# First norm's sums by token on ScalarE, rotary tables by token at the head: one change to a two-layer decoder trunk

## The chip, the cores and the metric

The kernel runs on one core of one Trainium2 chip. The metric is device time in microseconds of one execution of the whole program; a median over runs is given where there are several. Engines are named as in the profile: PE is TensorE, DVE is VectorE, ACT is ScalarE, POOL is GpSimd, SP is SyncE, which here only issues DMAs.

## What is computed

A decoder trunk of two layers over 512 tokens of width 1024, all positions at once, in fp32:

```
for i in range(2):
    h = rms_norm(x, norm_mix[i])
    proj = h @ w_in[i]            # split into parts A, B, C
    y_a = gated_delta_net(...)    # 4 heads of 64, causal conv of width 4
    y_b = mlstm(...)              # 4 heads of 64
    y_c = sliding_window_attention(..., cos, sin)   # 8 q heads, 2 kv heads
    x = x + concat(y_a, y_b, y_c) @ w_out[i]
    x = x + relu(rms_norm(x, norm_mlp[i]) @ w_up[i])**2 @ w_down[i]
    x = x + sigmoid(rms_norm(x, norm_ple[i]) @ w_ple_gate[i]) * (p[i] @ w_ple_proj[i])
return rms_norm(x, norm_final)
```

Two pieces matter here. `rms_norm` needs, for every token, the sum of the squares of its 1024 features. The rotary tables are cos and sin of position times frequency, with 8 frequencies; they turn the first 16 of the 64 features of each q and k head, and are the same in both layers.

## The kernel before

The residual is kept by feature: `X` is eight tiles of 128 features x 512 tokens, loaded from `xT` (L317, 256 KB each). Every fp32 product runs as three matmuls of high and low halves (`mm3`, L161): weights come from `wfm` in chunks of 256 KB (`w_load_`, L135) into the two buffers of `raw`, ACT rounds the high half (L141), POOL or DVE takes the difference (L143). A layer runs as follows.

- **Token-major projections** (tile `tok`, L313 to L319, `tok_mm`): for each of eight feature tiles, X is split into `xsh` (ACT, L190) and `xsl` (DVE, L191), a weight tile of 200 KB is loaded from `wtm` into the same two `raw` buffers (L260) and split into `whi` (ACT, L262) and `wlo` (DVE, L264), and PE issues 12 matmuls of 128x400.
- **First norm** (`Norm`, L194 to L226): `add` squares each X tile on ACT (L201, L204) and sums the squares over the eight tiles into `acc`, the first five sums on POOL and the last two on DVE (L205). `finish` sums over the 128 partitions by matmuls with a column of ones (tile `ss`, L212), works out rT = 1/sqrt(mean) with some ten tiny DVE operations of 128x4, and broadcasts it to all partitions as `R` (L220, L223). In layer 0 `add` is called in L321; later norms add while their X tiles are produced.
- **Gates, rows, conv** (L343 to L455): small DVE chains on the gate columns, then six projections for part A, each followed by a conv on DVE (tiles `craw`, `cc`).
- **Part A**: norms of k (tiles `psst`, `ssq`, `rk`, `cA`), decays, triangular systems (`At`), 16x16 inverses as a serial chain on DVE (`px`), doubling by small matmuls (the first is `t1p`, L564), scan over four blocks.
- **Part B** (`mql`, `mkS`, `me`, `pnm`), then **the rotary tables**, in layer 0 only (`rope_tables`, L231, called in L765): the positions are broadcast to 128 partitions x 512 tokens, and DVE works out the angle and its reduction for sin and cos on full 128x512 tiles (18 DVE operations); ACT's Sin follows (L248), and the tables go to DRAM (`rope_d`, L251). Both layers load them (L767, L770), multiply by R on POOL, and use them in `rope` (L775): shuffle and product on DVE, product and sum on POOL.
- **Part C**, output gates, output projection, then MLP and per-layer embedding, which are long runs of matmuls.

The order on each engine is not written by hand. A planner takes all instructions, ranks them by their place in the program, moved by offsets (`hp_` lifts by 200 places, `PRI` moves whole sections), and lays out a fixed order for each engine from durations of its own. On the chip each engine then runs its list in that order. All loads that this change touches go through SP's one queue.

Of the kernel before, what the change touches and what calls it, by code (L numbers as in the profile page):

```python
# [18 lines left out]
T = 512  # L19
D = 1024  # L20
# [6 lines left out]
# scheduling priority of (section, layer)  # L27
# [12 lines left out]
# columns of the packed constants  # L40
# [6 lines left out]
C_N = 552  # L47
# columns of the packed small weights of a layer
# [13 lines left out]
def trunk(ctx, tc, xT, pT, pos, wfm, wtm, consts, negi, smalls, gfin, out, dbg=None, depth=L):  # L62
# [41 lines left out]
    sc = cst[:, C_SC:C_SC + 8]  # L104
    for l in range(1, depth):
        nc.sync.dma_start(out=sm[l], in_=smalls[l])
# [63 lines left out]
    def rsqrt(y, x, shape, pool, tag):  # L170
        t = pool.tile(shape, F32, tag=tag + "w", name=tag + "w", bufs=2)
        V.tensor_scalar(t.bitcast(I32), x.bitcast(I32), 1, None, ALU.logical_shift_right)
        V.tensor_scalar(y.bitcast(I32), t.bitcast(I32), -1.0, MAGIC, ALU.mult, ALU.add)
        # one step of third order (8/3 too large), then one of Newton's that takes the factor back
        V.tensor_tensor(t, y, y, ALU.mult)
        V.tensor_tensor(t, t, x, ALU.mult)
        V.scalar_tensor_tensor(t, t, -10.0 / 3.0, t, ALU.add, ALU.mult)
        V.scalar_tensor_tensor(y, t, 5.0, y, ALU.add, ALU.mult)
        V.tensor_tensor(t, y, y, ALU.mult)
        V.scalar_tensor_tensor(t, t, -27.0 / 1024.0, x, ALU.mult, ALU.mult)  # L180
        V.scalar_tensor_tensor(y, t, 9.0 / 16.0, y, ALU.add, ALU.mult)
# [11 lines left out]

    class Norm:  # L194
        def __init__(self):
            self.acc = tp.tile([128, T], F32, tag="acc", name="acc", bufs=1)
            self.n = 0
# [10 lines left out]
        def finish(self, pt_=None):  # L208
            pt_ = pt_ or ps_tile
            ps = pt_([128, NB], "ss")  # L210
            for b in range(NB):
                PE.matmul(out=ps[:, b:b + 1], lhsT=self.acc[:, b * 128:(b + 1) * 128], rhs=ones[:, 0:1],  # L212
                          start=True, stop=True)
            ms = tp.tile([128, NB], F32, tag="ms", name="ms", bufs=2)
            V.tensor_scalar(ms, ps, 1.0 / D, EPS, ALU.mult, ALU.add)
            rT = tp.tile([128, NB], F32, tag="rT", name="rT", bufs=2)
            rsqrt(rT, ms, [128, NB], tp, "rn")
            pr = pt_([128, T], "rb")
            for b in range(NB):
                PE.matmul(out=pr[:, b * 128:(b + 1) * 128], lhsT=rT[:, b:b + 1].broadcast_to([128, 128]), rhs=ident,  # L220
                          start=True, stop=True)
            R = tp.tile([128, T], F32, tag="R", name="R", bufs=1)
            A.activation(out=R, in_=pr, func=ACTF.Copy)  # L223
            ri = tp.tile([128, NB], F32, tag="ri", name="ri", bufs=2)
            V.tensor_tensor(ri, ms, rT, ALU.mult)
            return rT, ri, R  # L226

# [1 line left out]
    rope_d = dp.tile([2, 128, T], F32, name="rope_d", bufs=1)  # L229

    def rope_tables(us):  # L231
        pi = us([128, T], "pi").bitcast(I32)
        nc.sync.dma_start(out=pi, in_=pos.broadcast_to([128, T]))
        ang = us([128, T], "ang")
        V.tensor_copy(ang, pi)
        V.tensor_scalar(ang, ang, sc[:, 0:1], None, ALU.mult)
        for dst, off in ((1, 0.0), (0, 0.25)):
            k = us([128, T], "k")
            V.tensor_scalar(k, ang, float(np.float32(1.0 / (2 * np.pi))), off, ALU.mult, ALU.add)
            V.tensor_scalar(k, k, ROUND, ROUND, ALU.add, ALU.subtract)  # L240
            r = us([128, T], "r")
            V.scalar_tensor_tensor(r, k, -PI2[0], ang, ALU.mult, ALU.add)
            for c in PI2[1:]:
                V.scalar_tensor_tensor(r, k, -c, r, ALU.mult, ALU.add)
            if off:
                V.tensor_scalar(r, r, float(np.float32(np.pi / 2)), None, ALU.add)
            V.tensor_scalar(r, r, PI_LO, -PI_LO, ALU.min, ALU.max)
            A.activation(out=k, in_=r, func=ACTF.Sin)  # L248
            if dst:
                V.tensor_scalar(k, k, sc[:, 1:2], None, ALU.mult)  # L250
            nc.sync.dma_start(out=rope_d[dst], in_=k)  # L251
            dump(("rope_c", "rope_s")[dst], k)
# [23 lines left out]
    nrm = Norm()  # L276

    for l in range(depth):
# [33 lines left out]
        # token-major projections: mv, sv, gates  # L312
        pst = [(ps_tile if b < 2 else pa_tile)([128, 400], "tok") for b in range(NB)]  # L313
        for k in range(8):
            if l == 0:
                with hp_():
                    nc.sync.dma_start(out=X[k], in_=xT[k])  # L317
                    XS[k] = split(X[k], xs, "xs", 18, s_l[:, S_GMIX + k:S_GMIX + k + 1])
            tok_mm(pst, k, *tok_weights(l, k))  # L319
        if l == 0:  # L320
            for m in range(8):  # L321
                nrm.add(m)
        with hp_():
            rT, rI, R = nrm.finish(pa_tile)
        dump(f"R{l}", R)
# [52 lines left out]
        # rows  # L378
# [45 lines left out]
        # GDN q, k, v: conv, silu  # L424
# [55 lines left out]
        # k, v token-major  # L480
# [13 lines left out]
        # decays and the lower-triangular systems  # L494
# [41 lines left out]
        # base inverses of 16 x 16, then 32 x 32  # L536
# [78 lines left out]
        # scan over blocks  # L615
# [83 lines left out]
        # c'_{J,I}: ig - bl + totals of blocks J..I-1  # L699
# [64 lines left out]
        if l == 0:  # L764
            rope_tables(us)  # L765
# [231 lines left out]
        if final:  # L997
            # the last row tiles by halves of the tokens, so that the first half's norm hides
# [66 lines left out]
def const_arrays():  # L1065
# [9 lines left out]
    d = i % 64  # L1075
    inv = np.float32(500000.0) ** (-np.arange(0, 16, 2, dtype=np.float32) / np.float32(16))
    cst[:, C_SC] = np.where(d < 16, inv.astype(np.float32)[d % 8], 0.0)
    cst[:, C_SC + 1] = np.where(d < 8, -1.0, np.where(d < 16, 1.0, 0.0))
# [9 lines left out]
def stationary(w, ks, ms):  # L1088
    # [K, M] -> tiles [128 (k), 128 (m)] in the order of use
# [7 lines left out]
def pack(x, p, positions, w_in, conv_w, gdn_a_log, gdn_dt_bias, gdn_norm, mlstm_i_bias, mlstm_f_bias, mlstm_norm,  # L1097
         attn_sinks, w_out, norm_mix, norm_mlp, w_up, w_down, norm_ple, w_ple_gate, w_ple_proj, norm_final):
    def a(v):
        return np.asarray(v)  # L1100

    xT = np.ascontiguousarray(a(x)[0].T.reshape(8, 128, T))
    pT = np.ascontiguousarray(a(p)[:, 0].transpose(0, 2, 1).reshape(L, 2, 128, T))
    pos = np.ascontiguousarray(a(positions).reshape(1, T))
# [42 lines left out]
    return dict(xT=xT, pT=pT, pos=pos, wfm=np.stack(fms), wtm=np.ascontiguousarray(np.stack(tms)), consts=cst, negi=neg,  # L1147
# [3 lines left out]
NAMES = ["xT", "pT", "pos", "wfm", "wtm", "consts", "negi", "smalls", "gfin"]  # L1151
# [17 lines left out]
```

## Time and profile before

| what | value |
|---|---|
| median of 3 runs | 1396.97 us (1394.41 to 1399.37) |
| profiled execution, first to last instruction | 1397.6 us |
| PE busy | 1352.9 us of it |
| DVE, ACT, POOL busy | 839.1, 599.4, 325.1 us |
| moved by DMA | 130.04 MB |

The profiled execution's own time is its span; nothing around it is recorded. A row of the timeline holds the start and the duration in us, engine, line, operation, tile written <- tiles read, and the engine's idle time before it with what ended it. In a row of groups, the numbers behind the bar are busy time in us and mean ns of one. A busy PE is not PE at its peak: the rows also show the TensorE clock that was granted.

### The profile page before, as it was taken

To read this page: it belongs to the slowest core of one execution; us is meant where nothing else is said; L and a number is where in the kernel's file an instruction comes from. 1 tells how busy PE (TensorE), PEld (TensorE's weight loads), DVE (VectorE), ACT (ScalarE), POOL (GpSimd) and SP (SyncE) were. 2 spreads that over 40 slices of the span, in tenths; PEclk is the share of its full clock that TensorE was granted. 3 is DMA by queue.
4 is the path that set the end of the run, shared out by engine and by line. 5 is a ranking of instruction groups with operands and counts; after the bars stand their busy time and mean duration, and the time that the engine had idled before them with its cause. 6 is when DMAs were issued, how large, how long until landed. Compare 5 with 4: busy or idle time off the path is not lost.

```text
span 1397.6 us, 20344 instructions
## 1 busy us (share of the span) xinstructions
PE 1352.9 (97%) x7334; PEld 1113.3 (80%) x7334; DVE 839.1 (60%) x1749; ACT 599.4 (43%) x1236; POOL 325.1 (23%) x302
## 2 busy tenths in 40 slices
PE   7999899999999999999999899999999999999996
PEld 7667788778888888888896678887888888888886
DVE  6877978674344444454758688886544434444555
ACT  5374354254243242443535545634433324234443
POOL 4443632362000000010235455326400000000112
PEclk9999989999999999999999999999999999999998
DMA  4333222233333333332433322212333333233332
GB/s 152 99 99 89 55 57 77 69 98 98 98 99 95 95 97 98 99 98 91 142 106 99 108 69 63 78 54 91 99 98 98 97 99 95 95 98 98 98 98 76
DMA packets 88596, 130.04 MB, mean 93 GB/s; under 512 B 21408, under 2 KB 30112, under 8 KB 88496
## 3 DMA queue, kind: packets, MB, share of 16 engines
q1 hardware_dynamic: 87408, 127.71, 30.0%
q8 instruction: 57, 0.93, 0.3%
q10 hardware_dynamic: 1088, 1.05, 0.2%
q14 instruction: 43, 0.35, 0.1%
HBM read 123.18 MB, written 5.54 MB: 92 GB/s over the span
## 4 chain that ended last, share of the span: by engine, by line
PE 80%; DVE 9%; ACT 3%; issue 3%; POOL 2%; DMA 1%; SPq 0%; DVEq 0%; POOLq 0%; ACTq 0%
PE down L166 8%; PE down L165 8%; PE down L167 8%; PE up L167 8%; PE up L165 8%; PE up L166 8%; PE proj L165 2%; PE proj L167 2%; PE proj L166 2%; PE gate L165 2%; PE gate L167 2%; PE gate L166 2%; PE outp L166 2%; PE outp L165 2%; PE outp L167 2%
## 5 line engine op out<-in xcount | busy, mean ns | idle before, releaser
L141 ACT ACTIVATE whi<-raw 128x512 fp32r<-128x512 f32 x404 | 253.3, 630 | 530.5 <-PE down L166 201.3
L143 DVE TENSOR_TENSOR wlo<-raw,whi 128x512 fp32r<-128x512 f32 x268 | 187.1, 700 | 132.9 <-ACT whi L141 132.6
L143 POOL TENSOR_TENSOR wlo<-raw,whi 128x512 fp32r<-128x512 f32 x136 | 185.2, 1364 | 203.8 <-ACT whi L141 191.9
L205 POOL TENSOR_TENSOR acc<-acc,sq 128x512 f32<-128x512 f32 x34 | 49.0, 1440 | 700.4 <-ACT sq L204 700.0
L167 PE MATMUL up<-xsh,wlo 128*128 128x512 f32 x512 | 199.4, 390 | 1.2 <-POOL wlo L143 1.2
L165 PE MATMUL up<-xsh,whi 128*128 128x512 f32 x512 | 199.6, 390 | 0.0
L166 PE MATMUL up<-xsl,whi 128*128 128x512 f32 x512 | 199.2, 389 | 0.0
L165 PE MATMUL down<-hidh,whi 128*128 128x512 f32 x512 | 199.2, 389 | 0.0
L166 PE MATMUL down<-hidl,whi 128*128 128x512 f32 x512 | 197.9, 389 | 0.0
L167 PE MATMUL down<-hidh,wlo 128*128 128x512 f32 x512 | 197.9, 389 | 0.0
L165 PE MATMUL proj<-xsh,whi 128*128 128x512 f32 x304 | 125.2, 412 | 9.0 <-DVE rdst L781 4.5
L167 PE MATMUL proj<-xsh,wlo 128*128 128x512 f32 x304 | 124.6, 410 | 5.3 <-POOL wlo L143 5.3
L166 PE MATMUL proj<-xsl,whi 128*128 128x512 f32 x304 | 123.4, 406 | 0.0
L167 PEld LDWEIGHTS up<-xsh,wlo 128*128 128x128 f32 x512 | 96.1, 188 | 22.7 <-POOL wlo L143 2.8
L165 PEld LDWEIGHTS down<-hidh,whi 128*128 128x128 f32 x512 | 96.1, 188 | 20.0
L167 PEld LDWEIGHTS down<-hidh,wlo 128*128 128x128 f32 x512 | 96.1, 188 | 20.0
L965 DVE TENSOR_TENSOR X<-X,down 128x512 f32<-128x512 f32 x64 | 44.0, 688 | 113.3 <-PE down L167 113.3
L165 PEld LDWEIGHTS up<-xsh,whi 128*128 128x128 f32 x512 | 96.1, 188 | 19.8
L166 PEld LDWEIGHTS down<-hidl,whi 128*128 128x128 f32 x512 | 96.1, 188 | 19.8
L166 PEld LDWEIGHTS up<-xsl,whi 128*128 128x128 f32 x512 | 96.1, 188 | 19.8
L956 DVE SCALAR_TENSOR_TENSOR ha<-up,R 128x512 f32<-128x512 f32 x64 | 44.1, 691 | 100.3 <-PE up L167 89.8
L165 PEld LDWEIGHTS proj<-xsh,whi 128*128 128x128 f32 x304 | 59.5, 196 | 25.2 <-DVE mql L689 4.3
(359 smaller groups left out, 2306.5 us busy)
## 6 DMA issues: line engine op xcount, KB each, us to landing
raw<-wfm SPq DMA_DIRECT2D x404, 256.0 KB, 2.6
X<-xT SPq DMA_DIRECT2D x16, 256.0 KB, 4.5
raw<-wtm SPq DMA_DIRECT2D x16, 200.0 KB, 2.4
gr<-scr SPq DMA_DIRECT2D x8, 256.0 KB, 4.4
Mr<-scr SPq DMA_DIRECT2D x8, 256.0 KB, 3.5
xd<-X SPq DMA_DIRECT2D x8, 256.0 KB, 2.0
X<-xd SPq DMA_DIRECT2D x8, 256.0 KB, 2.9
praw<-pT SPq DMA_DIRECT2D x2, 512.0 KB, 3.7
```

Source lines behind the costliest of these rows:

```text
L141: A.activation(out=hi, in_=raw, func=ACTF.Copy)
L143: (G if (i % NCH) * WC < WPOOL else V).tensor_tensor(lo, raw, f(hi), ALU.subtract)
L165: PE.matmul(out=ps, lhsT=wh, rhs=ah, start=start and k == 0, stop=False)
L166: PE.matmul(out=ps, lhsT=wh, rhs=al, start=False, stop=False)
L167: PE.matmul(out=ps, lhsT=wl, rhs=ah, start=False, stop=stop and k == n - 1)
L205: (G if self.n < 6 else V).tensor_tensor(self.acc, self.acc, q, ALU.add)
L956: V.scalar_tensor_tensor(a_t, ps, 0.0, R, ALU.max, ALU.mult)
L965: V.tensor_tensor(X[m], X[m], ps, ALU.add)
```

## The change

- **Sums of squares.** The host passes x a second time, by token (`xK`, four blocks of 128 tokens x 1024 features, 512 KB each). `token_sums` loads the four blocks into tile `xk` (two buffers, shared with `px` and others) and lets ACT square each with a running sum, so that the sums of 128 tokens come out as one column. In layer 0 the eight squares, the seven sums on POOL and DVE and the `ss` matmuls go; all other norms stay.
- **Rotary tables.** Positions come as 128 x 4 instead of 1 x 512. Angles, reduction and Sin are worked out by token on 128x32 and 128x64 tiles; then, for cos and sin each, POOL fills a 128x512 tile with the constant for unturned features, DVE puts the 8 frequencies into four places, PE transposes four 128x128 blocks to features x tokens, ACT copies the result out of PSUM, and the table goes to `rope_d` as before. The call moves from ahead of part C to just behind the first norm of layer 0.
- The constants get 8 columns of frequencies and lose two that were per feature. Comments were dropped, which changes no instruction.

```diff
+    def token_sums(raw):
+        ss = tp.tile([128, NB], F32, tag="sst", name="sst", bufs=1)
+        for b in range(NB):
+            x_b = raw([128, D], "xk")
+            nc.sync.dma_start(out=x_b, in_=xK[b])
+            A.activation(out=x_b, in_=x_b, func=ACTF.Square, accum_out=ss[:, b:b + 1])
+        return ss
...
-        def finish(self, pt_=None):
-            pt_ = pt_ or ps_tile
+        def sums(self, pt_):
             ps = pt_([128, NB], "ss")
...
+        def finish(self, pt_=None, ps=None):
+            pt_ = pt_ or ps_tile
+            ps = self.sums(pt_) if ps is None else ps
...
-    def rope_tables(us):
-        pi = us([128, T], "pi").bitcast(I32)
-        nc.sync.dma_start(out=pi, in_=pos.broadcast_to([128, T]))
-        ang = us([128, T], "ang")
...
+    def rope_tables(us, small):
+        pi = small([128, NB], "pi").bitcast(I32)
+        nc.sync.dma_start(out=pi, in_=pos)
+        pf = small([128, NB], "pf")
+        V.tensor_copy(pf, pi)
+        ang = small([128, NB, 8], "ang")
+        V.tensor_tensor(ang, pf.unsqueeze(2).broadcast_to([128, NB, 8]), fr.unsqueeze(1).broadcast_to([128, NB, 8]),
+                        ALU.mult)
+        k = small([128, 2, NB, 8], "rk2")
+        for j, off in ((0, 0.25), (1, 0.0)):
+            V.tensor_scalar(k[:, j], ang, float(np.float32(1.0 / (2 * np.pi))), off, ALU.mult, ALU.add)
+        V.tensor_scalar(k, k, ROUND, ROUND, ALU.add, ALU.subtract)
+        r = small([128, 2, NB, 8], "rr2")
+        for j in range(2):
+            V.scalar_tensor_tensor(r[:, j], k[:, j], -PI2[0], ang, ALU.mult, ALU.add)
+        for c in PI2[1:]:
+            V.scalar_tensor_tensor(r, k, -c, r, ALU.mult, ALU.add)
+        V.tensor_scalar(r[:, 0], r[:, 0], float(np.float32(np.pi / 2)), None, ALU.add)
+        V.tensor_scalar(r, r, PI_LO, -PI_LO, ALU.min, ALU.max)
+        A.activation(out=k, in_=r, func=ACTF.Sin)
+        for j in range(2):
+            src = us([128, NB, 128], "rsrc")
+            G.memset(src, 1.0 - j)
+            src4 = src.rearrange("p b (h e f) -> p b h e f", h=2, f=8)
+            for h in range(2):
+                for e in range(2):
+                    V.tensor_scalar(src4[:, :, h, e, :], k[:, j], -1.0 if j and not e else 1.0, None, ALU.mult)
+            pt = mm_tile("prt")
+            for b in range(NB):
+                PE.transpose(pt[:, b * 128:(b + 1) * 128], src[:, b, :], ident)
+            tab = us([128, T], "rtab")
+            A.activation(out=tab, in_=pt, func=ACTF.Copy)
+            nc.sync.dma_start(out=rope_d[j], in_=tab)
...
+        with hp_():
+            rT, rI, R = (nrm or Norm(False)).finish(pa_tile, None if nrm else token_sums(ws))
         if l == 0:
-            for m in range(8):
-                nrm.add(m)
-        with hp_():
-            rT, rI, R = nrm.finish(pa_tile)
+            rope_tables(us, tt)
...
-        if l == 0:
-            rope_tables(us)
```

More of the change, by code (lines that the diff above doesn't have):

```diff
@@ L46 @@
 C_SC = 544
-C_N = 552
+C_FR = 552
+C_N = 560
 S_CONV = 0
@@ L61, in trunk @@
 @with_exitstack
-def trunk(ctx, tc, xT, pT, pos, wfm, wtm, consts, negi, smalls, gfin, out, dbg=None, depth=L):
+def trunk(ctx, tc, xT, xK, pT, pos, wfm, wtm, consts, negi, smalls, gfin, out, dbg=None, depth=L):
     nc = tc.nc
@@ L104, in trunk @@
     sc = cst[:, C_SC:C_SC + 8]
+    fr = cst[:, C_FR:C_FR + 8]
     for l in range(1, depth):
@@ L192, in split, with __init__ @@
         return hi, lo
+    def token_sums(raw):
[5 more added lines that the diff above has]
+        return ss
     class Norm:
-        def __init__(self):
-            self.acc = tp.tile([128, T], F32, tag="acc", name="acc", bufs=1)
+        def __init__(self, acc=True):
+            self.acc = acc and tp.tile([128, T], F32, tag="acc", name="acc", bufs=1)
             self.n = 0
@@ L213, in finish @@
                           start=True, stop=True)
+            return ps
+        def finish(self, pt_=None, ps=None):
+            pt_ = pt_ or ps_tile
+            ps = self.sums(pt_) if ps is None else ps
             ms = tp.tile([128, NB], F32, tag="ms", name="ms", bufs=2)
@@ L229, in trunk @@
     rope_d = dp.tile([2, 128, T], F32, name="rope_d", bufs=1)
-    def rope_tables(us):
-        pi = us([128, T], "pi").bitcast(I32)
-        nc.sync.dma_start(out=pi, in_=pos.broadcast_to([128, T]))
-        ang = us([128, T], "ang")
[L235 to L252, printed above, removed]
@@ new lines, in rope_tables @@
+    def rope_tables(us, small):
[31 more added lines that the diff above has]
+            nc.sync.dma_start(out=rope_d[j], in_=tab)
+            dump(("rope_c", "rope_s")[j], tab)
@@ L275, in trunk @@
     XS = [None] * 8
-    nrm = Norm()
+    nrm = None
     for l in range(depth):
@@ L319, in trunk @@
             tok_mm(pst, k, *tok_weights(l, k))
+        with hp_():
+            rT, rI, R = (nrm or Norm(False)).finish(pa_tile, None if nrm else token_sums(ws))
+        dump(f"R{l}", R)
         if l == 0:
-            for m in range(8):
-                nrm.add(m)
-        with hp_():
-            rT, rI, R = nrm.finish(pa_tile)
-        dump(f"R{l}", R)
+            rope_tables(us, tt)
         seg('tok')
@@ L1074, in const_arrays @@
     cst[64:, C_IND + 1] = 1.0
-    d = i % 64
     inv = np.float32(500000.0) ** (-np.arange(0, 16, 2, dtype=np.float32) / np.float32(16))
-    cst[:, C_SC] = np.where(d < 16, inv.astype(np.float32)[d % 8], 0.0)
-    cst[:, C_SC + 1] = np.where(d < 8, -1.0, np.where(d < 16, 1.0, 0.0))
+    cst[:, C_FR:C_FR + 8] = inv.astype(np.float32)[None]
     cst[:, C_SC + 2] = np.where(i < 4, 1.0, -1.0)
@@ L1102, in pack @@
     xT = np.ascontiguousarray(a(x)[0].T.reshape(8, 128, T))
+    xK = np.ascontiguousarray(a(x)[0].reshape(NB, 128, D))
     pT = np.ascontiguousarray(a(p)[:, 0].transpose(0, 2, 1).reshape(L, 2, 128, T))
-    pos = np.ascontiguousarray(a(positions).reshape(1, T))
+    pos = np.ascontiguousarray(a(positions).reshape(NB, 128).T)
     fms, tms, sms = [], [], []
@@ L1146, in pack @@
     gfin = np.ascontiguousarray(a(norm_final).reshape(8, 128).T)
-    return dict(xT=xT, pT=pT, pos=pos, wfm=np.stack(fms), wtm=np.ascontiguousarray(np.stack(tms)), consts=cst, negi=neg,
+    return dict(xT=xT, xK=xK, pT=pT, pos=pos, wfm=np.stack(fms), wtm=np.ascontiguousarray(np.stack(tms)), consts=cst, negi=neg,
                 smalls=np.stack(sms), gfin=gfin)
-NAMES = ["xT", "pT", "pos", "wfm", "wtm", "consts", "negi", "smalls", "gfin"]
+NAMES = ["xT", "xK", "pT", "pos", "wfm", "wtm", "consts", "negi", "smalls", "gfin"]
 def kernel(**inputs):
```

## The prediction

> **What bounds the kernel now.** I read the page first, then stretches of the two layers side by side, then what PE waits for, then the DVE timeline of the head and the groups of the rotary tables.
>
> ```profile
> span 1397.6 us, 20344 instructions
> PE 1352.9 (97%) x7334; PEld 1113.3 (80%) x7334; DVE 839.1 (60%) x1749; ACT 599.4 (43%) x1236; POOL 325.1 (23%) x302
> ```
>
> PE is the bound of the whole, so only what frees PE, or adds to it, counts. The change touches layer 0 up to its part C alone. Both layers' mixing parts, 0 to 290 us and 700 to 970 us, hold the same work but for the head loads and the tables:
>
> ```profile
> core 0: us, PE busy (x) PEld busy (x) DVE busy (x) ACT busy (x) POOL busy (x), PEclk, DMA share, GB/s
> 0.00:290.00 290.00, 267.31 (x1778) 215.52 (x1778) 223.94 (x567) 139.68 (x358) 122.31 (x122) 0.96 0.30 89
> 700.00:970.00 270.00, 262.12 (x1808) 212.45 (x1806) 208.81 (x546) 130.60 (x343) 117.06 (x114) 0.97 0.28 83
> 160.00:180.00 20.00, 15.20 (x65) 11.62 (x63) 19.41 (x53) 6.33 (x20) 11.39 (x10) 0.91 0.24 55
> ```
>
> The columns are length and busy times. PE's idle time is 290.0 - 267.3 = 22.7 us in layer 0 and 270.0 - 262.1 = 7.9 us in layer 1; DVE is busier in layer 0 by 15.1 us. From 160 to 180 us DVE is full (19.4 of 20) and PE idles 4.8 us. The waits of PE in 0 to 290 us, total, times and longest:
>
> ```profile
> PE proj L165 <- DVE rdst L781: 4.5, 2, 2.9
> PE tok L272 <- DVE wlo L264: 3.7, 2, 2.2
> ```
>
> Both are waits for DVE: one in the head (tok), one at 160 to 180 us (the rope products of part C). The change aims at work that stands ahead of each.
>
> **The head.** DVE's timeline there, and POOL's:
>
> ```profile
> 9.39 2.50 DVE L191 SCALAR_TENSOR_TENSOR xsl<-X,sm,xsh 128x512 fp32r<-128x512 f32 x2 [0.90 <-ACT xsh L190]
> 11.82 2.08 DVE L264 TENSOR_TENSOR wlo<-raw,whi 128x400 fp32r<-128x400 f32 x1
> 13.82 3.46 DVE L191 SCALAR_TENSOR_TENSOR xsl<-X,sm,xsh 128x512 fp32r<-128x512 f32 x2
> 18.01 0.57 DVE L264 TENSOR_TENSOR wlo<-raw,whi 128x400 fp32r<-128x400 f32 x1
> 18.57 1.40 DVE L191 SCALAR_TENSOR_TENSOR xsl<-X,sm,xsh 128x512 fp32r<-128x512 f32 x2
> ...
> 12.19 4.55 POOL L205 TENSOR_TENSOR acc<-acc,sq 128x512 f32<-128x512 f32 x3
> ...
> 13.92 8.51 SPq L260 DMA_DIRECT2D raw<-wtm  x4
> ```
>
> While POOL adds squares, DVE's pairs of xsl take 2.50 and 3.46 us instead of 1.40, and wlo 2.08 instead of 0.57: 1.10 + 2.06 + 1.51 = 4.7 us lost. The change removes those POOL sums, so this DVE time returns. It matters because the third wlo frees a `raw` buffer: it ends at 13.9 us, and only then, at 13.92, SP issues the fifth wtm load; PE then waits for that tile's wlo, too. The transfers of that time:
>
> ```profile
> 10.00:12.00 2.00, 2.00 (x13) 2.00 (x12) 2.00 (x3) 2.00 (x5) 2.00 (x2) 1.00 1.04 379
> 12.00:14.00 2.00, 0.52 (x4) 0.19 (x2) 2.00 (x2) 2.00 (x5) 1.92 (x3) 1.00 0.14 44
> 14.00:16.00 2.00, 2.00 (x11) 2.00 (x12) 2.00 (x2) 0.84 (x2) 1.92 (x2) 1.00 0.36 102
> 16.00:20.00 4.00, 1.76 (x10) 1.42 (x9) 4.00 (x10) 1.58 (x3) 0.73 (x1) 0.95 0.09 17
> 20.00:24.00 4.00, 4.00 (x16) 3.97 (x15) 2.66 (x5) 1.07 (x2) 0.00 (x0) 0.62 0.47 135
> ```
>
> Up to 12 us the DMAs are full (1.04 share, 379 GB/s); from 12 to 20 us they are nearly empty (44, 102, 17 GB/s). After the two waits the granted clock in 20 to 24 us is 0.62, which costs another 4.0 x 0.38 = 1.5 us. So the head can return at most 3.7 + 1.5 = 5.2 us. Against it stands the second load of the input, 4 x 512 KB = 2.10 MB, 5.5 us at 379 GB/s, 1.4 us for each block, on the queue on which the wtm loads go. The gap of 8 us holds it, but a wtm load issued behind a block lands later by up to 1.4 us, and the fifth wtm load, now earlier, will meet the first two blocks. Bounds 0 and -5.2; I take the middle, **-2.5**.
>
> PE's own work there: the `ss` matmuls go, eight transposes come.
>
> ```profile
> 26.25 0.80 PE ss L212 x8
> 779.29 0.67 PE psst L461 x4
> ```
>
> That is -0.8, and 2 x 0.67 = +1.3 for two sets of four transposes (the same fp32 blocks of 128x128): **+0.5**.
>
> ACT: eight squares go, four squares of 128x1024 come. The rows of seven of the eight, of the reading of a running sum, and of the wait that tells how full ACT is:
>
> ```profile
> L204 ACT ACTIVATE sq<-X 128x512 f32<-128x512 f32 x7 | 4.1, 614 | 0.0
> L834 ACT ACTIVATION_READ_ACCUMULATOR srr<-srr,snm 128x1 f32 x64 | 12.0, 188 | 0.0
> L262 ACT ACTIVATE whi<-raw 128x400 fp32r<-128x400 f32 x8 | 4.3, 533 | 8.3 <-DMA raw<-wtm 5.3 <-PE tok L273 3.0
> ```
>
> No row shows that square; two of 614 ns and the reading of the sum, 188 ns, bound it at 1.42 us, one of 614 ns below. 4 x (0.6 to 1.4) = 2.5 to 5.7 us against 4.9 (8 x 0.614): even. ACT idles 8.3 us ahead of `whi` in this stage, which covers it. If that cover is gone, 0.8 us.
>
> **The tables.** What leaves the stage at 93 to 115 us, by its five largest groups:
>
> ```profile
> L244 DVE SCALAR_TENSOR_TENSOR r<-k,r 128x512 f32<-128x512 f32 x6 | 4.1, 684 | 0.0
> L240 DVE TENSOR_SCALAR k<-k 128x512 f32<-128x512 f32 x2 | 1.8, 916 | 0.0
> L242 DVE SCALAR_TENSOR_TENSOR r<-k,ang 128x512 f32<-128x512 f32 x2 | 1.4, 678 | 0.0
> L247 DVE TENSOR_SCALAR r<-r 128x512 f32<-128x512 f32 x2 | 0.9, 428 | 0.0
> L239 DVE TENSOR_SCALAR k<-ang 128x512 f32<-128x512 f32 x2 | 0.8, 424 | 0.0
> ```
>
> These alone are 9.0 us of DVE. PE does not wait at that place; the question is whether DVE, relieved, is earlier at 160 to 180 us where PE does wait. Layer 1, which has no tables, gives a measure: from the norm of k (`ssq`) to the first doubling matmul (`t1p`).
>
> ```profile
> 94.85 0.19 DVE L463 TENSOR_SCALAR ssq<-psst 128x32 f32<-128x32 f32 x1
> 779.98 0.19 DVE L463 TENSOR_SCALAR ssq<-psst 128x32 f32<-128x32 f32 x1 [0.64 <-PE psst L461]
> 183.31 4.00 PE t1p L564 x128
> 858.61 3.86 PE t1p L564 x128
> ```
>
> Layer 0 takes 183.3 - 94.9 = 88.5 us, layer 1 858.6 - 780.0 = 78.6: 9.8 us longer, close to the 9.0 of DVE. But the two layers have other section offsets, and the wait that is certain to be tied to DVE is only the 4.5 us on `rdst`. Bounds 0 and -9.8. I take **-5**, near the row of the wait: once `rdst` is early, the serial DVE chain of the 16x16 inverses is next to be late.
>
> What comes instead: 12 operations on 128x4 to 128x64 and eight copies into the 128x512 tile, 20 in all. The nearest rows, one with POOL quiet and one with POOL busy:
>
> ```profile
> L176 DVE TENSOR_TENSOR rkw<-rkw,skc 128x16 f32<-128x16 f32 x1 | 0.2, 161 | 0.0
> L175 DVE TENSOR_TENSOR rkw<-rk 128x16 f32<-128x16 f32 x1 | 1.3, 1280 | 0.0
> ```
>
> 20 x 0.16 = 3.2 us, in a stage where DVE is busy only 2.66 of 4 us (20 to 24 us) and gets 4.7 back: **0**. If the cover is gone (the planner lays them into the gate chain behind the head), +3.2, and the slow form would add 1.1 for each hit.
>
> ACT's two table switches go along:
>
> ```profile
> 100.00 1.28 ACT L248 ACT_TABLE_LOAD   x1
> 115.36 1.28 ACT L724 ACT_TABLE_LOAD   x1
> 116.66 0.40 ACT L724 ACTIVATE me<-MrD,mcc 128x128 f32<-128x128 f32 x1
> ```
>
> Each costs 1.28 us, and the next activation starts 1.30 us after the load. At the head the second switch stands ahead of the gates' tanh. Bounds 0 and 2 x 1.28 = +2.6; with the idle of ACT there I take **+0.5**. The Trainium skill speaks against the move here (ScalarE: Activation LUTs, What ACT_TABLE_LOAD costs): every switch is given there as 1283 ns of load plus about 1380 ns of drain, some 2.66 us. By that page the upper bound would be +5.3 and not +2.6. The trace agrees with the load, but shows no drain behind it.
>
> **Sum.** -2.5 + 0.5 - 5 + 0 + 0.5 = -6.5 us on 1397.6, so 1391.1. The span stands 0.6 above the median of the runs, 1396.97, so the forecast on the median is **1390.5**. Best by the bounds: -5.2 + 0.5 - 9.8 = -14.5, 1382.5. Worst: 0 + 0.5 + 0 + 3.2 + 2.6 + 0.8 = +7.1, 1404.1. A measurement of this kernel can tell about 0.3%, 4.2 us, from no change.
>
> **Rivals.**
>
> *Layer 0 becomes like layer 1.* The whole 9.8 us of the stage and the whole 5.2 of the head return: 1382.5. For it: the difference of the stages is nearly the DVE time removed, and idle PE in layer 0 exceeds layer 1's by 14.8 us. Against it: other offsets, and the head's loads collide.
>
> *The relief is covered.* PE has independent matmuls from 93 to 160 us, so DVE's earlier end moves only where PE spends its idle time; or the planner lays the tables elsewhere than at the head, as it already pulls the call of L765 up to 93 us, far ahead of its text. Then the head's gain and the added work cancel: -2.5 + 0.5 + 0.5 and nothing more, 1395.5, and anything from 1393 to 1401.
>
> *The input's second copy holds the weights.* One queue, in order: if the planner issues blocks ahead of the fifth to eighth wtm load, these wait behind 2.10 MB, PE waits for `wlo` as it does now, and then runs at a low clock. Price: 5.5 us more waiting and 1.5 us more of low clock, 7.0, and term one is zero: 7.0 + 0.5 + 0.5 = +8.0. It decides as soon as the relief of the tables returns less than 3.8 us (8.0 - 4.2); with none it is 1405. For it: the DMAs are full up to 12 us, just when the fifth load would now start. Against it: 8 nearly empty us follow, and the loads of wtm are lifted in rank as the blocks are, and stand ahead of them in the program.
>
> **Chances.** Forecast 0.42 (of it 0.04 ends within 0.3%), like layer 1 0.18, covered 0.23, held weights 0.17. Faster by over 0.3%: 0.38 + 0.18 = 0.56; within: 0.23 + 0.04 = 0.27; slower: 0.17. The range for 8 in 10 goes from 1381, just past the best case, to 1401, which takes in the covered case and leaves out most of the third rival. The forecast and the first rival, which hold most of the chance, go from 1382 to 1394.
>
> **What would show it.** Head right: xsl pairs near 1.40 us, wlo near 0.57, no wait of `tok` on `wlo` over 1 us, clock near 1.00 where it was 0.62, `tok` done by 27 us or so. Wrong: PE or ACT waiting for wtm or `xk`. Tables right: no wait on `rdst`, `ssq` to `t1p` near 83 us. If that stage stays near 88 us, the relief was covered and the forecast is wrong; if `t1p` is early but the MLP does not start earlier, the gain was given back in the scan. If the gate chain shows the table switch or the 20 small operations ahead of `craw`, the zeros above were wrong.

## The result, and the profile after

The change makes the kernel slower: 1414.61 us in the median (1413.56 to 1420.52) against 1397.81 us for the kernel before in the same measurement, ratio 1.0125, 95% interval 1.0101 to 1.0148. The forecast was 1390.5 us. The profiled execution's span went from 1397.6 to 1411.5 us, by 13.9. (Three executions in the experiments below, of 1500.80, 4667.91 and 6673.14 us, are left out of the ratios, though not of the medians.)

The page of the kernel after, totals and the two long groups of the MLP:

```profile
span 1411.5 us, 20338 instructions
...
PE 1367.3 (97%) x7334; PEld 1113.2 (79%) x7334; DVE 825.2 (58%) x1749; ACT 601.4 (43%) x1237; POOL 317.9 (23%) x299
...
L167 PE MATMUL down<-hidh,whi 128*128 128x512 f32 x512 | 202.3, 395 | 0.0
L169 PE MATMUL down<-hidh,wlo 128*128 128x512 f32 x512 | 201.0, 395 | 0.0
...
L167 PE MATMUL up<-xsh,whi 128*128 128x512 f32 x512 | 199.8, 390 | 0.0
```

The same two groups of the kernel before (its helper stands two lines higher):

```profile
L165 PE MATMUL down<-hidh,whi 128*128 128x512 f32 x512 | 199.2, 389 | 0.0
...
L165 PE MATMUL up<-xsh,whi 128*128 128x512 f32 x512 | 199.6, 390 | 0.0
```

DVE is relieved by 13.9 us (839.1 to 825.2) and POOL by 7.2, as meant. But PE, the bound, is busy 14.4 us longer with the same 7334 matmuls. Most of that is in a part that the change does not touch: a matmul of `down` takes 395 ns in place of 389, one of `up` 390 as before. The mean of one counts its tail, which overlaps the next matmul; from start to start the mean step of `down` went from 226.7 to 233.3 ns. Each of the eight stretches of `down`, 192 matmuls each, takes 44.80 us in place of 43.52: 8 x 1.28 = 10.2 us. The stages of `gate`, which reads hidden tiles too, and of `ple`, whose inputs lie in the same pool, take another 1.8.

Where the 13.9 us arise, from the starts of the stages in the two traces:

| part | before | after | difference |
|---|---|---|---|
| start to the first `up` of layer 0 | 291.6 | 291.3 | -0.3 |
| first `up` to last `down`, both layers | 710.4 | 720.8 | +10.4 |
| gates and embedding, both layers | 113.4 | 115.2 | +1.8 |
| mixing of layer 1 | 266.1 | 268.7 | +2.6 |
| tail | 16.1 | 15.5 | -0.6 |

The 2.6 us in layer 1 are not put down to anything: with the tiles in step (below) that part comes out between 0.8 less and 1.9 more than before. So there are two findings to explain: why untouched matmuls step slower, and why the end of layer 0's mixing, which the forecast had 6.5 us earlier, is only 0.3 us earlier.

**The head did what was said.** DVE's timeline there:

```profile
8.82 1.41 DVE L193 SCALAR_TENSOR_TENSOR xsl<-X,sm,xsh 128x512 fp32r<-128x512 f32 x2
10.14 0.57 DVE L292 TENSOR_TENSOR wlo<-raw,whi 128x400 fp32r<-128x400 f32 x1
10.63 1.50 DVE L193 SCALAR_TENSOR_TENSOR xsl<-X,sm,xsh 128x512 fp32r<-128x512 f32 x2
```

Pairs of `xsl` at 1.41 and 1.50 us, `wlo` at 0.57, where POOL had stretched them to 2.50, 3.46 and 2.08. The stretches of time:

```profile
12.00:14.00 2.00, 2.00 (x13) 2.00 (x12) 1.28 (x3) 1.50 (x3) 0.00 (x0) 1.00 1.03 415
14.00:16.00 2.00, 1.94 (x11) 1.60 (x9) 1.01 (x6) 1.34 (x5) 0.00 (x0) 1.00 1.08 332
16.00:20.00 4.00, 3.48 (x19) 3.48 (x20) 2.85 (x13) 3.12 (x5) 0.00 (x0) 1.00 0.88 331
```

PE is busy where it idled, at a clock of 1.00, and the second copy of the input fills the DMAs (331 to 415 GB/s) without holding the weights: `tok` ends at 27.8 us in place of 31.5. At the first `craw` 2.3 us of this are left (38.5 against 40.8). What comes in between:

```profile
28.95 0.47 ACT L363 ACTIVATE V65m<-tok,r2T 128x256 f32<-128x256 f32 x1
29.30 0.64 ACT L143 ACTIVATE whi<-raw 128x512 fp32r<-128x512 f32 x1
...
31.29 0.65 ACT L278 ACTIVATE rtab<-prt 128x512 f32<-128x512 f32 x1
31.95 1.28 ACT L372 ACT_TABLE_LOAD   x1
31.96 0.33 SPq L279 DMA_DIRECT2D rope_d<-rtab  x1
33.24 0.21 ACT L372 ACTIVATE beta<-Gt 128x16 f32<-128x16 f32 x1
...
33.97 0.62 ACT L143 ACTIVATE whi<-raw 128x512 fp32r<-128x512 f32 x1
35.98 5.31 SPq L139 DMA_DIRECT2D raw<-wfm  x3
```

The copy of the table (0.65) and the table switch (1.28) stand on ACT ahead of `beta` and of the third `whi`; the store of the table stands on SP's queue ahead of the weights. DVE needs `beta` for the chain of the gates; after, and before:

```profile
33.49 0.17 DVE L373 TENSOR_SCALAR beta<-beta 128x16 f32<-128x16 f32 x1 [4.99 <-ACT beta L372]
...
34.95 0.65 DVE L346 TENSOR_SCALAR beta<-beta 128x16 f32<-128x16 f32 x1 [2.40 <-ACT beta L345]
```

DVE waits 4.99 us where it waited 2.40, so its chain starts only 1.5 us earlier, and `craw` stands behind it. There 1.4 of the 3.7 us go. PE itself waits only 0.4 us for weights here. The rest is gone by 60 us: the 97th matmul of `proj` starts at 59.7 us, before at 59.6. On that way PE has a granted clock of 0.84 from 50 to 60 us, where it had 1.00.

**The tables' relief ends at one wait.** The inverses (`px`) end at 167.2 us in place of 173.0, the last load of `XB`, which brings them back, is issued by 172.7 in place of 178.5: 5.8 us, somewhat more than the 5 taken. But `t1p` starts only 3.2 us earlier (180.0, 183.2), and PE's waits up to 300 us now read:

```profile
PE proj L169 <- POOL wlo L145: 4.6, 3, 3.5
PE proj L167 <- ACT srr L859: 4.6, 1, 4.6
...
PE proj L167 <- DVE rdst L806: 0.2, 1, 0.2
```

The 4.6 us on `wlo` lie elsewhere than at the head but for 0.4: the longest of them, 3.5, ends at 70.7 us, where the kernel before waited 2.4 and 1.5. Two waits of `proj`, 4.5 us together, went by the name of `rdst` before; one of 4.6 us goes by that of `srr` now. The rows of ACT, DVE and PE around it show what it is:

```profile
158.65 0.37 ACT L848 ACTIVATE srr<-psc 128x256 f32<-128x256 f32 x1
169.30 0.40 ACT L859 ACTIVATE srr<-srr,snm 128x128 f32<-128x128 f32 x1 [10.29 <-DVE snm L856]
...
170.09 0.61 ACT L143 ACTIVATE whi<-raw 128x512 fp32r<-128x512 f32 x1
...
170.89 0.67 DVE L806 TENSOR_TENSOR rdst<-proj,RC 128x512 f32<-128x512 f32 x1
...
171.70 0.77 PE L167 MATMUL proj<-xsh,whi 128*128 128x512 f32 x1 [4.58 <-ACT srr L859]
```

And in the kernel before:

```profile
171.49 0.68 DVE L781 TENSOR_TENSOR rdst<-proj,RC 128x512 f32<-128x512 f32 x1
...
172.31 0.47 PE L165 MATMUL proj<-xsh,whi 128*128 128x512 f32 x1 [2.95 <-DVE rdst L781]
```

The exp of the first attention scores waits 10.29 us for `snm` from DVE, which is still full (19.39 of 20 us at 160 to 180, as before 19.41). Behind it in ACT's fixed order stands `whi`, the next weights for PE. But these are ready at 170.7, and PE starts at 171.70, 0.14 us after the end of `rdst` (171.56), just as in the kernel before (172.17 and 172.31). In the built program this matmul waits for two things, `whi` and the `rdst` that reads its buffer last. The exp of `srr` happens to end at the same moment, 171.57. So PE still waits for `rdst`, which ends 0.6 us earlier than before, though the inverses end 5.8 earlier. Its input is ready at 160.4, but up to 170.3 DVE works on what stands ahead of it: the inverses, the norm of part B and, for 3.9 us, the first scores (`srr`, `smx`, `snm`, `ses`), which stood behind it before. The expectations of the runs in step below still take this wait for one on `srr`, and those that speak of a 3.5 us wait on `wlo` behind `tok` mean the one at 70.7 us.

```profile
0.00:290.00 290.00, 269.15 (x1779) 216.55 (x1780) 213.70 (x567) 141.33 (x359) 115.38 (x119) 0.95 0.32 95
...
160.00:180.00 20.00, 14.48 (x54) 10.91 (x53) 19.39 (x43) 7.77 (x25) 13.26 (x12) 0.74 0.23 54
```

Up to 290 us PE idles 20.8 us, before 22.7. What the clock takes I worked out by slices of 10 us, each slice's busy time by one minus its granted clock: 11.9 us up to 290, before 10.9. Idle -1.9, clock +1.0, and +0.4 for the transposes less the `ss` matmuls make -0.5; measured is -0.3 at the first `up`.

### The profile page after: what moved, and what is told of

Read it like the earlier page. It is cut to its first block, busy times and chain, and to the rows that moved or that the text cites. A ratio compares the mean times of both kernels' runs of the same rounds, so it can differ in the third digit from the quotient of the medians.

```text
span 1411.5 us, 20338 instructions
## 1 busy us (share of the span) xinstructions
PE 1367.3 (97%) x7334; PEld 1113.2 (79%) x7334; DVE 825.2 (58%) x1749; ACT 601.4 (43%) x1237; POOL 317.9 (23%) x299
## 4 chain that ended last, share of the span: by engine, by line
PE 82%; DVE 8%; ACT 3%; issue 2%; POOL 2%; DMA 2%; SPq 0%; DVEq 0%; ACTq 0%; POOLq 0%
PE down L169 8%; PE down L167 8%; PE down L168 8%; PE up L169 8%; PE up L167 8%; PE up L168 8%; PE proj L167 3%; PE proj L169 3%; PE proj L168 3%; PE gate L167 2%; PE gate L169 2%; PE gate L168 2%; PE outp L168 2%; PE outp L167 2%; PE outp L169 2%
## 5 line engine op out<-in xcount | busy, mean ns | idle before, releaser
L167 PE MATMUL down<-hidh,whi 128*128 128x512 f32 x512 | 202.3, 395 | 0.0
L169 PE MATMUL down<-hidh,wlo 128*128 128x512 f32 x512 | 201.0, 395 | 0.0
L168 PE MATMUL down<-hidl,whi 128*128 128x512 f32 x512 | 200.9, 395 | 0.0
L216 POOL TENSOR_TENSOR acc<-acc,sq 128x512 f32<-128x512 f32 x29 | 41.6, 1435 | 707.2 <-ACT sq L215 707.0
```

What stands on the lines that cost most here:

```text
L167: PE.matmul(out=ps, lhsT=wh, rhs=ah, start=start and k == 0, stop=False)
L168: PE.matmul(out=ps, lhsT=wh, rhs=al, start=False, stop=False)
L169: PE.matmul(out=ps, lhsT=wl, rhs=ah, start=False, stop=stop and k == n - 1)
L216: (G if self.n < 6 else V).tensor_tensor(self.acc, self.acc, q, ALU.add)
```

## The experiments

**Theory A**: the step of back-to-back matmuls depends on where the moving tile starts in a partition relative to the stationary one. The constants are 8 columns wider, which moves all that lies above by 32 bytes, and the 16 bytes of the new sums, padded to 32, lie between the weights and the hidden tiles. So weights (`whi`) went from 40384 to 40416, hidden tiles (`hidh`) from 108224 to 108288, and their distance from 67840 to 67872. The inputs of `up` (`xsh`) stay 14336 above the weights. **Theory B**: the matmuls of the MLP are slower because of what goes ahead of them or runs beside them (clock, traffic), or because of where the tiles stand as such.

These runs bear on it; distance is `hidh` less `whi`, from the built programs, and step is the mean of `down` from start to start in the trace (a stretch divided by its 192 matmuls; the expectations below differ from it by up to 0.5 ns):

| kernel | whi | hidh | distance | over a multiple of 256 | step, ns |
|---|---|---|---|---|---|
| before | 40384 | 108224 | 67840 | 0 | 226.7 |
| after | 40416 | 108288 | 67872 | 32 | 233.3 |
| after, hidden +32 | 40416 | 108320 | 67904 | 64 | 229.0 |
| before, hidden +32 | 40384 | 108256 | 67872 | 32 | 233.3 |
| before, all +32 | 40416 | 108256 | 67840 | 0 | 226.7 |
| before, hidden +64 | 40384 | 108288 | 67904 | 64 | 229.0 |
| after, hidden +96; sums only; tables late | 40416 | 108384 | 67968 | 128 | 233.3 |
| tables only | 40416 | 108256 | 67840 | 0 | 226.7 |
| after, sums only and tables late, in step | 40448 | 108288 | 67840 | 0 | 226.7 |
| after, hidden +224 | 40416 | 108512 | 68096 | 0 | 226.7 |

### The hidden tiles shifted, in both kernels

In the kernel after, and in the same way in the kernel before (+ 8, and + 16 for the +64), a tile below the hidden ones is made wider; only the first columns are used:

```diff
-            self.acc = acc and tp.tile([128, T], F32, tag="acc", name="acc", bufs=1)
+            self.acc = acc and tp.tile([128, T + 8], F32, tag="acc", name="acc", bufs=1)[:, 0:T]
```

For "all +32", the kernel before gets 8 unused columns of constants and nothing else:

```diff
-C_N = 552
+C_N = 560
```

> The changed kernel with the tile acc widened by 8 columns (32 bytes), so that the tiles behind it, hid among them, start 32 bytes later; the order on every engine is that of the changed kernel. Theory A (a matmul is slower where its weights tile and its moving tile start at different places modulo 64 bytes: in the changed kernel whi starts at 32 and hid at 0 modulo 64): down falls from 233.4 ns a step back to 226.6, the gate's matmuls too; 1536 x 6.7 ns = 10.3 us for down and about 1.5 us for the gate, so 1402 to 1404 us. Rival B (hid is slow by itself when it does not start where it did before, 64 modulo 128): down stays at 233 or so, 1414 us. Rival C (the larger input traffic or the earlier schedule slows the MLP): nothing changes, 1414 us.

> The kernel before with acc widened by 32 bytes: whi stays at 0 modulo 64, hid moves to 32; nothing else changes. Theory A: down goes from 226.6 to 233 ns a step, plus 10 to 12 us, 1408 to 1410 us. Rival B (hid slow away from 64 modulo 128): the same rise. Rival C (traffic or schedule): 1397 us, unchanged.

> The kernel before with the constants 8 columns wider, so that the weight tiles, xs and hid all start 32 bytes later: whi, xs and hid all at 32 modulo 64. Theory A: no matmul changes, 1397 us. Rival B (hid slow by itself away from its old place): down at 233 ns, 1408 us. A variant, in which any start off a multiple of 64 bytes is slow, gives up, proj and down all slower, plus 20 us and more.

> The kernel before with acc widened by 64 bytes: hid at 0 modulo 128 instead of 64, exactly its address in the changed kernel (108288); whi stays at 0 modulo 64. Theory A with 64 as the modulus: unchanged, 1397 us, down at 226.6 ns. Theory A with 128 as the modulus, and rival B: down at 233 ns, 1408 us.

Measured: after, hidden +32: 1411.33 us, ratio to before 1.0085 (1.0054 to 1.0117). Before, hidden +32: 1410.85, 1.0085 (1.0061 to 1.0108). Before, all +32: 1398.78, 1.0001 (0.9989 to 1.0014). Before, hidden +64: 1403.81, 1.0040 (1.0019 to 1.0062).

With the kernel before and 32 bytes alone, nothing of the change in it, the step is that of the kernel after, and the time goes up by 0.85%. With the same 32 bytes ahead of weights and hidden tiles alike there is no difference. And hidden tiles at one and the same place, 108288, step at 233.3, 229.0 or 226.7 ns, by where the weights are. That rules out the change's schedule and the absolute place, and theory B with them. My idea of the pattern was wrong, though: I had taken a distance of a multiple of 64 for fast, and it gave 229.0 ns, in both kernels alike.

### How far the pattern repeats

The same edit in the kernel after with 24 columns more (+96 bytes), and with 56 (+224):

```diff
-            self.acc = acc and tp.tile([128, T], F32, tag="acc", name="acc", bufs=1)
+            self.acc = acc and tp.tile([128, T + 24], F32, tag="acc", name="acc", bufs=1)[:, 0:T]
```

> The changed kernel with acc widened by 96 bytes, so that hid starts at the same place modulo 128 as whi and xs (96); order as in the changed kernel. Theory A, now with 128 as the modulus (difference 0: 226.6 ns a step, 64: 228.6, 32: 233.2): down back at 226.6 ns, 3 us below e1. What is left against the kernel before is then the price of the schedule alone: 1400 us if the layers' mixing parts are as in the profile of the changed kernel (+2 us), up to 1408 us if the runs of e1 at 1410 to 1414 us come from its schedule. Rival: the rest of the slow-down is in the matmuls too, and the time falls to 1397 us.

> The kernel after with the norm's tile of sums 56 columns wider, so that the hidden tiles start 224 bytes further: difference to the weights 68096 bytes, 256 more than before. Nothing is left out. What is still open is how far the pattern repeats: differences 0 and 256 over a multiple of 2048 gave 226.6 ns, 288 gave 233.2, 320 gave 228.6 and 384 gave 232.8. If it repeats every 256 bytes: down 226.6 ns and a time like that of the run with the sums placed ahead of the weights, within 2 us. If only the two differences seen are fast (the position within 2048 counts): down between 228 and 234 ns and a time of 1405 to 1417.

Measured: +96 gives 1417.09 us, 1.0137 (1.0112 to 1.0163), step 233.3: a multiple of 128 is not enough either. +224 gives a step of 226.7 and 1405.49 us, 1.0052 (1.0033 to 1.0071). So distances of 256 and 512 over a multiple of 2048 are fast, and 288, 320 and 384 are not; a repeat of 256 bytes fits all of them, and the 14336 of `up` as well (0 over a multiple of 2048). The time is 1 to 3 us above the 1402.7 and 1404.4 of the version in step (below), where at most 2 were expected.

### The other operand

In the kernel before, 32 unused bytes between the weights and all above them:

```diff
+    gp = ctx.enter_context(tc.tile_pool(name="gp", bufs=1))
+    gap = gp.tile([128, 8], F32, name="gap")
+    V.memset(gap, 0.0)
     xs = ctx.enter_context(tc.tile_pool(name="xs", bufs=1))
```

> The kernel before with an unused tile of 32 bytes between the weight buffers and all that lies above them, so that the streams xsh and xsl, which feed up and the projections, start 14368 bytes above the weights in place of 14336, and the hidden tiles 67872 in place of 67840. Instructions are the same but for one memset. Nothing is left out. Theory A (difference of starts): now both up and down step at about 233 ns in place of 226.6, each of the sixteen stretches 1.3 us longer, so some 21 us for them, 1 to 2 for the gates, and a few for the projections in the mixing: 1420 to 1430. Rival (it is something of the hidden tiles alone, their bank or their writers): up stays at 226.6 ns and the time is about 1410, as with the hidden tiles alone shifted.

> The kernel before with 32 unused bytes between the weight buffers and the streams, once more, for a profile at the usual clock; the first one's ran at a clock of 0.19. Nothing is left out. Theory A (difference of starts): the groups of up go from a mean of 389 ns to 395 as those of down did, each stretch of up 44.8 us in place of 43.5, down the same: time 1420 to 1428. Rival (something of the hidden tiles alone): up stays at 389 to 390 ns and the time, 1426, comes from the mixing.

Measured: 1425.72 us, 1.0192 (1.0171 to 1.0214), and again 1423.08, 1.0160 (1.0114 to 1.0207). The groups of the second:

```profile
L168 PE MATMUL up<-xsh,whi 128*128 128x512 f32 x512 | 202.6, 396 | 0.0
...
L168 PE MATMUL down<-hidh,whi 128*128 128x512 f32 x512 | 202.2, 395 | 0.0
```

Now `up` is slow too, and each of its later stretches takes 44.8 us like those of `down`. A 32-byte tile that nothing reads costs 22 to 27 us, 1.6 to 1.9%. Theory A stands: it is not something of the hidden tiles, since the inputs of `up` at such a distance cost the same.

### The parts alone

*Sums only* takes the old rotary tables back, *tables only* the old sums, *tables late* calls the new tables where the old ones stood. The first and third have the pad of +96 in them, which I then held to be in step; so they are out of step.

```diff
         if l == 0:
-            rope_tables(us, tt)
...
         seg('rope')
+        if l == 0:
+            rope_tables(us, tt)
```

> Only the sums by token on ACT with the second load of the input; the tables as before at their old place; all tiles in the same phase as in e5. Theory S1 (the head gains, as forecast, and the tables' move spoils it through the table switch, the copies and the late weights behind it): tok ends near 27 us as in the changed kernel, no wait of 3.5 us on wlo behind it, 1393 to 1396 us. Theory S2 (what the head gains is given back anyway, since a later stage of layer 0 waits for DVE): the MLP of layer 0 starts within 1 us of 291, 1397 to 1399 us.

> Only the tables by token at the head; the sums as before; all tiles in the same phase. S1: the head's cost without its gain: beta waits behind a table load, 1398 to 1403 us. S2 (the relief of DVE is given back before the MLP): At and the inverses 5 to 7 us earlier, MLP of layer 0 not earlier than 290 us, 1396 to 1399 us. My forecast's term of -5 would give 1392 to 1394 us.

> The whole change, in phase, but the new tables are called at the old place, ahead of part C. S1: no table load ahead of beta, no wait on wlo of 3.5 us behind tok; the small tables still spare DVE some 6 us at 93 to 115 us: 1392 to 1396 us. S2: as e5, within 2 us. If the planner pulls the tables forward to the head by itself, the profile shows rsrc there and the run equals e5.

Measured: sums only 1410.01, 1.0100 (1.0071 to 1.0129); tables only, in step by itself, 1400.77, 1.0022 (1.0007 to 1.0036); tables late 1412.35, 1.0106 (1.0082 to 1.0129). Neither half is faster than the kernel before. The first `up` starts at 289.8, 291.3 and 292.7 us (before 291.6): no half brings the MLP forward by more than 1.8 us. The first and the third were expected at 1392 to 1399 us or, for tables late, at the 1417 of the +96; out of step, their times settle neither theory. Tables only lies in the 1398 to 1403 of S1, and its trace has both sides of it: `ssq` to `t1p` takes 83.2 us in place of 88.5, but `ssq` itself comes 3.2 us late (98.0 against 94.8).

### The change in step

The sums are allocated with the constants, below the weights, so that all moves together:

```diff
-        ss = tp.tile([128, NB], F32, tag="sst", name="sst", bufs=1)
+        ss = cp.tile([128, NB], F32, name="sst")
```

It was run twice, once as a control for what follows, and once each with the sums only and with the tables late.

> The kernel after with one tile placed elsewhere: the 128x4 sums of the token blocks are allocated with the constants, ahead of the weight buffers, so that weights and hidden tiles move together and their difference is 67840 bytes, as in the kernel before. Nothing is left out. Theory A (the matmuls' step follows the difference between the start of the stationary tile and of the moving tile): down back at 226.6 ns, each of its eight stretches 43.5 us, so 10 to 12 us less than after, 1402 to 1404.5 by its median 1414.6, or 1400 to 1403 if the layers' waits fall well. Theory B (the MLP is slow because of what the change does ahead of it: clock, heat or traffic): down stays at 233 ns and the time within 4 us of 1414.6. What is left over 1398 is then the price of the schedule: the ACT wait on srr that took the place of rdst, and the proj waits on wlo.

> The whole change in step, the same kernel as the first run in step, as the control of this call. Nothing is left out. 1400 to 1405. If the spells of 10 us at a clock of 0.50, seen at 125 to 135 us in its first trace while TensorE was busy, belong to this order of work: again about half of the runs show a mean clock of 0.979 or less and are 5 to 8 us longer than the others. If they were chance of that chip and hour: few do, and the time is 1397 to 1400.

> Only the first half of the change: the input by token and its sums on ACT, with the rotary tables worked out as before, late in layer 0. The 128x4 sums are allocated with the constants, so that the difference of weights and hidden tiles is 67840 bytes as before. Nothing is left out. Theory (each half's own price, without the shift of the tiles): the head returns some 2 us at tok and the MLP is not slowed, down 226.6 ns: 1394 to 1398, against 1398 for the kernel before and 1410 for the same half out of step. Rival (the head's gain is given back wholly before the MLP): first up at 291 to 292 us and the time 1398 to 1400.

> The whole change with the new tables worked out at their old place in the program, late in layer 0, and the sums placed with the constants, so that the tiles are in step. Nothing is left out. If the place of the tables at the head is what costs (the table switch ahead of beta, the load of rope_d ahead of the weights): 1396 to 1399, level with the kernel before or faster. If it is not: 1400 to 1404, like the whole change in step.

| in step | us | ratio to before |
|---|---|---|
| whole change | 1402.66 | 1.0025 (1.0007 to 1.0043) |
| whole change, again | 1404.41 | 1.0037 (1.0018 to 1.0055) |
| sums only | 1397.41 | 1.0007 (0.9983 to 1.0031) |
| tables late | 1400.35 | 1.0004 (0.9987 to 1.0021) |

One allocation brings back 10 to 12 of the 16.8 us. The order of instructions on every engine is the same as in the kernel after. What is left, 3.5 to 5.2 us, belongs to the new order of work. In its first trace the first `up` starts at 298.7 us, 7.4 later than in the trace of the kernel after, though order and work are the same. From 100 to 140 us:

```profile
100.00:120.00 20.00, 19.91 (x105) 14.92 (x105) 13.64 (x39) 8.60 (x20) 5.74 (x5) 1.00 0.31 83
120.00:140.00 20.00, 20.00 (x79) 15.11 (x78) 7.49 (x22) 4.64 (x14) 4.39 (x5) 0.66 0.14 36
```

And the kernel after in the same slices:

```profile
100.00:120.00 20.00, 19.74 (x104) 14.38 (x103) 12.49 (x34) 7.85 (x19) 4.92 (x5) 1.00 0.29 78
120.00:140.00 20.00, 20.00 (x111) 15.57 (x110) 12.03 (x31) 10.27 (x30) 6.46 (x7) 1.00 0.23 54
```

PE is busy throughout in both, yet in one execution its clock is 0.66 over 20 us, and 79 matmuls are done in place of 111. Up to 290 us, idle time and what the clock takes account for the difference in these four to within 1 us:

| up to 290 us | PE idle | lost to the clock | first `up` | first `up` less both |
|---|---|---|---|---|
| before | 22.7 | 10.9 | 291.6 | 258.0 |
| after | 20.8 | 11.9 | 291.3 | 258.6 |
| in step | 20.7 | 19.4 | 298.7 | 258.6 |
| in step, tables late | 23.1 | 11.4 | 292.1 | 257.6 |

The count is rough: for the sums only in step, with 16.6 us idle and 24.8 lost to the clock, it leaves 253.6.

In the first run in step six executions have a mean clock of 0.979 or less and take 1404.2 to 1406.7 us; the other six take 1396.4 to 1401.1. In the second run it is seven of twelve, as expected, but with 1402.4 to 1409.8 against 1401.9 to 1404.0 they are not 5 to 8 us apart. Over both runs in step and the +224 it is 18 of 30, for the kernel before 5 of 81, for tables only and for tables late in step 0 of 12 each. With the tables at their old place the low clocks are gone, and the ratio is 1.0004; the median, 1400.35, is 4 us under the control's of the same call, yet still in the 1400 to 1404 that was named for the case that the place does not matter. So it is likely, not shown, that the rest of the price lies in the place of the tables. The low clocks are not tied to the place of the tables alone, though: for the sums only in step it is 9 of 12, with a time level with before. The spells seem to go with an order of work as a whole. The expectation named the table switch and the store at the head as what the move would cost; the trace of tables late has 2.4 us more idle PE than the first one in step, not less, and 8.0 us less lost to the clock. What sets off a spell stays open. In the trace in step the clock falls at 125 us amid short matmuls (`pkq`, `pnm`), with no idle time of PE in the 10 us before it (as far as the profile can tell, which models the ends of matmuls), and the same matmuls in the trace of the kernel after keep the clock. The Trainium skill (TensorE: Matmul & The Clock Gate, Part 1: The HAM clock gate) lowers the clock after a window of some 3.4 us in which PE is idle; this trace shows no such window ahead of the fall.

### The wait on srr taken away

This run takes the label `srr` of the long wait at its word. The first two blocks of scores are raised in rank, so that DVE forms `snm` ahead of the last three steps of the inverses:

```diff
         for un in units:
-            pend.append((un, scores(*un)))
+            with hp_(300 if l == 0 and un in ((0, 0), (1, 0)) else 0):
+                pend.append((un, scores(*un)))
```

> The whole change in step, with the first two blocks of attention scores raised in rank by 300, so that DVE forms snm ahead of the last three steps of the inverses and the exp of srr no longer stands on ACT ahead of the weights with 10.5 us to wait. The order on PE changes with it (psc some projections earlier). Nothing is left out. Theory (the relief of the tables is given back at this one wait): the wait of proj on srr, 4.6 us, falls under 1, the doubling starts 3 to 4.6 us earlier than in the same kernel without the rank, and the time is 3 to 5 us less than that of the control of this call. Rival (DVE is full there, so that whatever goes first, another waits as long): proj waits 3 to 5 us on something else, rdst or the inverses, and the time is within 1.5 us of the control.

Measured: 1425.52 us, ratio to before 1.0182 (1.0150 to 1.0215), 21 us more than the control. PE's waits up to 310 us:

```profile
PE ptv L882 <- DVE spc L877: 2.3, 1, 2.3
PE psc L844 <- DVE srr L851: 1.8, 1, 1.8
PE proj L167 <- DVE rdst L806: 1.7, 1, 1.7
```

The wait that went by the name of `srr` is gone, and 5.8 us of waits on DVE stand in its place, 1.7 of them on `rdst`: the rival's case at this wait. `t1p` starts at 190.4 us in place of 186.4. The idle time up to 290 us is 21.0 us against 21.4 of the control. But neither side foresaw 21 us more. The planner's order changed in layer 1 as well, and there, from 910 to 940 us, PE is granted 0.50 to 0.64 of the clock: from the start of the last `down` stretch of layer 0 to the next `up` it takes 388.3 us, the control 366.1. By the count above, 18.8 of these 22.2 us are lost to the clock. So this run shows that the wait goes on elsewhere on DVE, and its time shows how much a new order can cost through the clock; it is no measure of the 4.6 us.

## Why the prediction was wrong

- **The sum had no term for where tiles lie.** "PE's own work there" was costed for `ss` and the transposes, and every other matmul was taken as unchanged. The constants' 8 columns and the 16 bytes of sums were read as free. They cost 10.2 us at `down` and 1.8 at the gates in the profiled execution, and one allocation moved to the constants took them back. This is the step that failed first, and the largest: 10 to 12 of the 16.8 us. It does not turn the sign alone: without it the change is still 0.25 to 0.37% slower, at the edge of what can be told from no difference, and not the 6.5 us faster that were forecast. That rest is the next two points and the clock.
- **The tables, -5.** Right to the inverses (5.8 us earlier), wrong at `rdst`. The step was "once `rdst` is early, the serial DVE chain of the 16x16 inverses is next to be late"; it was the other way round. DVE is as full as before, the new order puts the first scores ahead of the second `rdst`, and this ends 0.6 us earlier, with 4.6 us of waiting for 4.5. This is the rival "The relief is covered", by DVE's own order rather than by independent work. `ssq` to `t1p` is 180.0 - 93.7 = 86.3 us, between the 83 and the 88 that were named for the two cases.
- **The head, -2.5.** Right in place and size at first: 3.7 us at the end of `tok`, 2.3 at the first `craw`. It was not seen that PE has lost it by 60 us, in part to the wait for `beta`. The prediction had named a table switch in the gate chain as a sign that its zeros were wrong. The sums alone, in step, idle 6.1 us less than the kernel before up to 290 us, but lose 24.8 us to the clock where that loses 10.9; they start `up` 3.4 us later in that trace and are level in the median.
- **The small operations, 0; the squares, even.** The square of 128x1024 took 1.06 us, reading its sum 0.19, within the bounds of 0.6 to 1.4. The transposes took 0.60 each four, 0.67 had been taken.
- **The table switch, +0.5.** It does stand ahead of `beta`, as feared, and with the copy of the table puts the third `whi` at 33.97. The two take 1.4 of the head's 3.7 us, more than the 0.5 taken. The switch took 1.28 us, and the next activation started 1.29 us after its start: no drain behind it, as the prediction had read the trace against the Trainium skill (ScalarE: Activation LUTs, What ACT_TABLE_LOAD costs).
- **The rivals.** "The input's second copy holds the weights", the only one with a slower end, did not occur: full DMAs, no wait of `tok` on weights over 1 us. The result lies beyond its 1405, and above the worst sum of bounds, 1404.1, which the change in step just about reaches. No bound could hold a cost that had no term.
- **The clock** was priced once, at the head (1.5 us). It is worth as much as the whole forecast: spells at 0.50 cost 7.5 us between two executions of one order.

## What to carry to other kernels

When an edit adds or widens a tile, compare the starts of the operands of the long runs of matmuls before and after, and the step of those matmuls in the trace; a group that the edit does not touch and whose mean moved by 1.5% is the first sign. Keep small new tiles below the pair (or pad to keep the distance). A relief is worth only what the next late instruction on each in-order queue leaves of it: read the queue of the engine that feeds the bound, not only the waits of the bound. And where an instruction waits for two things, the profile names one: set its start beside the end of each.

## What the runs showed of the hardware

- Back-to-back matmuls of 128x512 in fp32 halves step at 226.7 ns when moving and stationary tile start a multiple of 256 bytes apart, at 229.0 ns with 64 more, at 233.3 with 32 or 128. The absolute start did not matter (40384, 40416 and 40448 for the weights, 108288 for hidden tiles at three steps). Why is not shown. The Trainium skill (SBUF — State Buffer, Who interferes with whom) says that "PE and ACT never wait on anyone"; it also calls PE's two read ports independent. These runs show that the distance between PE's own two operands can cost 3%.
- With PE busy throughout, the granted clock fell to 0.50 for some 14 us in one execution (0.76 and 0.56 in the slices of 120 to 130 and 130 to 140 us) and not in another of the same order of instructions (1.00).
